# Order of the PSUM banks: the second products of four FFNs and an output projection visit their accumulators bank by bank

## The chip, the cores and the metric

The kernel is one program on one core of a Trainium2 chip. Its engines are TensorE (PE, with its weight load PEld), VectorE (DVE), ScalarE (ACT), GpSimd (POOL) and SyncE (SP), each with a queue of its own that is worked off in order; they wait for each other on semaphores. PE writes its products into PSUM, which has eight banks; a bank holds one tile of 128 x 512 fp32 numbers. The metric is the device time of one execution in microseconds (us), as the median of several runs.

## The reference

A decoder trunk of two layers on one sequence of 256 tokens with 1024 channels, in fp32. Every layer computes

```
h += 1/2 * SwiGLU(RMSNorm(h)); h += Mixer(RMSNorm(h)); h += 1/2 * SwiGLU(RMSNorm(h))
SwiGLU(x) = (silu(x @ w_in[:, :2816]) * (x @ w_in[:, 2816:])) @ w_out
```

The mixer of layer 0 is an S5 state-space mixer. After layer 0 one shared set of keys and values is computed. The mixer of layer 1 is an attention with three branches (16 heads in four groups of four): compressed keys, selected blocks, and a window. The sum of its branches, 256 x 1024, is multiplied by `w_o` (1024 x 1024) and added to h. So the program has four FFNs with inner width 2816, and one output projection of 256 x 1024 by 1024 x 1024.

## The kernel before

**Products.** Tokens are two tiles t of 128 rows. An fp32 product is made of three fp32r matmuls (`mm3`, L112-117): both operands are split into a high part and a low remainder, and hi·hi (L115), hi·lo (L116) and lo·hi (L117) are added in one PSUM bank. The activations stand still in the array (128 x 128), the weights move through (128 x 512).

**Weights.** They arrive by DMA in granules of 1 MB from SP's queue (`load_granule`, two `raw` buffers). `split_half` makes the high part on ACT (`whi`, L86, or L96 with a gain) and the low part on DVE (`wlo`, L92 or L99). The weights `w_o` of the output projection are fetched with `eng='ag'`: there POOL subtracts (`wlo`, L92 on POOL). `whi` and `wlo` have five buffers each that are used in turn, so the cast into a buffer waits until PE has done the last matmul with what the buffer held.

**FFN** (`ffn`, L177-242). The inner width is worked in 11 chunks of 256. For one chunk the first products go to two banks `mm` (one per token tile); ACT and DVE make g = silu · gate of them (L235, L236); PE transposes g (L190), and `split` makes its hi and lo parts `gT` (L140, L141). `second(c, gT)` multiplies by the chunk of `w_out` and adds to `acc2`, four PSUM tiles `o{t}{hf}` (token tile t, half hf of the channels), which stay open over all 11 chunks. It visits them by f (half of the chunk), hf, t; in the last chunk by t, hf, f, since there DVE adds a finished half to h (L214) and `done` starts the next stage. The pool `ps_a` hands out the banks 4, 5, 6, 7 in the order in which the tiles are asked for: o00, o01, o10, o11. In visiting order o00, o10, o01, o11 the banks are 4, 6, 5, 7.

**Attention** (L796-964) is a list of units, `ORD` (L794): queries, `logits` (l), `compressed` (c), `mix` (m) by group and token tile, and `project` (p). `compressed` makes the softmax over the compressed keys: after ACT's exponential (L856) and DVE's normalisation (L862) it splits the weights into `pst` (ACT L140, DVE L141), which PE transposes (`tr<-ident,pst`, L868) and ACT copies into `pcT` (L869). `mix` normalises the weights `Pt` of a token tile by eight DVE operations (L906), transposes them on PE (L913) and multiplies them with the values (L922, L925). The last units are `c3 p0 p2 m30 p4 m31 p6`.

**Projection** (`project`, L933-946). p0, p2, p4, p6 each add two slabs of 128 channels to four accumulators: `acc[0]` is a bank `mm` (0) and a bank `x` (7), `acc[1]` a bank `mm` (1) and a bank `x` (6); the second index is the half n of the channels. A unit visits them by t, n, j (j the slab), that is six matmuls in a row to one bank. After the last unit DVE adds them to h (L945).

**What sets the order.** The code is recorded, and a scheduler orders each engine's queue by modelled times and by `tc.issue_after`; what stands in a row in the program is therefore not what stands in a row in the code, and a small change of one engine's order can change another's. At run time each engine goes through its queue in that fixed order.

Of the kernel before, what the change touches and what calls it, by code (L numbers as in the profile page):

```python
# [9 lines left out]
F32 = mybir.dt.float32  # L10
# [6 lines left out]
P = 128  # L17
D = 1024
KT = D // P
# [13 lines left out]
def kernel(ctx: ExitStack, tc: tile.TileContext, A, out):  # L33
# [16 lines left out]
    def tr_bank():  # L50
        return Banks.tr.tile([P, 512], F32, name=Banks.tag)

    # ---- constants and gains
    h = pers.tile([P, 2, D], F32, name="h")
    ident = pers.tile([P, P], F32, name="ident")
    gains = pers.tile([P, 6, KT], F32, name="gains")
# [4 lines left out]
    nc.sync.dma_start(out=h[:, 0, :], in_=A["x"][0])  # L61
    nc.sync.dma_start(out=gains, in_=A["gains"])

    # ---- weights: each granule is split exactly into hi + lo parts as it arrives, scaled by the gain of its rows
    class Last:
        dma = act = dve = pe = None

# [8 lines left out]
    nc.sync.dma_start(out=raw0[:, 1024:2048], in_=A["w_in1_0"][0, 0][:, 1024:2048])  # L76

    def split_half(raw, j, w, gain, k0, eng="av"):
        """eng: which engines round and subtract"""
        eh, el = ({"a": S, "v": V, "g": G}[x] for x in eng)  # L80
        hi = hip.tile([P, 1024], F32R, name="whi")[:, 0:2 * w]
        lo = lop.tile([P, 1024], F32R, name="wlo")[:, 0:2 * w]
        r = raw[:, j * 2 * w:(j + 1) * 2 * w]
        if gain is None:
            if eh is S:
                Last.act = S.activation(hi, r, AF.Copy)  # L86
            else:
                Last.dve = V.tensor_copy(hi, r)
        for s_ in range(2):
            c = slice(s_ * w, (s_ + 1) * w)  # L90
            if gain is None:
                i = el.tensor_tensor(out=lo[:, c], in0=r[:, c], in1=hi[:, c].bitcast(F32), op=ALU.subtract)  # L92
            else:
                g_ = gains[:, gain, k0 + s_:k0 + s_ + 1]
                if eh is S:
                    Last.act = S.activation(hi[:, c], r[:, c], AF.Identity, scale=g_)  # L96
                else:
                    V.tensor_scalar(out=hi[:, c], in0=r[:, c], scalar1=g_, scalar2=None, op0=ALU.mult)
                i = V.scalar_tensor_tensor(out=lo[:, c], in0=r[:, c], scalar=g_, in1=hi[:, c].bitcast(F32), op0=ALU.mult, op1=ALU.subtract)  # L99
            if el is V:  # L100
                Last.dve = i
        return hi, lo
# [14 lines left out]
        Last.pe = T.matmul(ps, lhsT=xl, rhs=wh, start=False, stop=stop_)  # L117

    def gemm(acc, xT, gen, kts=KT, lead=False):
        """acc[t] = x[t] @ W over kts slabs; lead: token tile 0 goes first in groups of four slabs"""  # L120
        for k0 in range(0, kts, 4):
            ws = [next(gen) for _ in range(4)] if lead else None
            for t_ in range(2) if lead else (None,):
                for k in range(k0, k0 + 4):
                    w = ws[k - k0] if lead else next(gen)
                    for t in ((t_,) if lead else range(2)):
                        mm3(acc[t], xT, k, t, w, k == 0, k == kts - 1)

    # ---- 1/rms of the rows of one token tile of h, from its two halves
    def row_square(hc, t, hf, ss):  # L130
        junk = small.tile([P, 512], mybir.dt.bfloat16, name="junk", bufs=1)
        S.activation(junk, hc[:, t, hf * 512:(hf + 1) * 512], AF.Square, scale=1.0 / 32.0, accum_out=ss[:, 2 * t + hf:2 * t + hf + 1])
# [8 lines left out]
        V.tensor_tensor(out=dst_lo, in0=src, in1=dst_hi.bitcast(F32), op=ALU.subtract)  # L141
        return i

    # ---- h^T as hi and lo parts, channels on partitions, with 1/rms of its rows
    class Acts:
        def __init__(self, hc):
            self.h = hc
# [16 lines left out]
                    row_rstd(u, self.ss, self.rs)  # L164

    def background(bg, n):
        """n steps of other work, queued behind what has been issued so far"""
        if bg is None:
            return
        with ExitStack() as st:  # L170
            for i in (Last.act, Last.dve, Last.dma):
                st.enter_context(tc.issue_after(i.ins))
            for _ in range(n):
                next(bg, None)

    # ---- res += 1/2 SwiGLU(rmsnorm(h)); done(t, half) once a half of token tile t of res is complete
    def ffn(x, gi, w_in, w_out, res, perm=False, bg=None, steps=1, done=None, first=()):  # L177
        with tc.tile_pool(name="ffn", bufs=2) as fp, tc.tile_pool(name="ps_a", bufs=1, space=PSUM) as pa:
            xT, rs = x.xT, x.rs
            acc2 = [[pa.tile([P, 512], F32, name=f"o{t}{hf}") for hf in range(2)] for t in range(2)]  # L180
            g_in = granules([w_in[c, kh] for c in range(NCH) for kh in range(2)], gain=gi, first=first)
            g_out = granules([w_out[j] for j in range(NCH)])

            def transposed(g):
                """g^T of one chunk, hi and lo, tokens in natural order"""
                gT = fp.tile([P, 2, 2, 256], F32R, name="gT")
                ps = tr_bank()
                for f in range(2):
                    for t in range(2):
                        T.transpose(ps[:, (f * 2 + t) * P:(f * 2 + t + 1) * P], g[:, t, f * P:(f + 1) * P], ident)  # L190
                if perm:
                    src = ps.rearrange("p (f t e c) -> p f t e c", f=2, t=2, e=2)
                    hi, lo = (gT[:, i].rearrange("p f (c t e) -> p f t e c", t=2, e=2) for i in range(2))
                    for f in range(2):
                        split(hi[:, f], lo[:, f], src[:, f])
                else:
                    split(gT[:, 0], gT[:, 1], ps.rearrange("p (f c) -> p f c", f=2))
                return gT
# [42 lines left out]
                background(bg, steps)  # L241
            second(NCH - 1, transposed(prev))

    # ---- S5 in chunks of four tokens: discretisation, rotation tables, and stationary operands
    BG1 = 2
    NG = 32
    NC = 64
# [3 lines left out]
    def s5_prepare(kp, sp, W):  # L251
# [34 lines left out]
        yield  # L286

        def exp_parts(x):
            """2^n and exp(r) - 1 with x = n ln2 + r."""
            xc = ts(nt(), x, -87.0, ALU.max, 88.0, ALU.min)  # L290
            t = ts(nt("et"), xc, LOG2E, ALU.mult, MAGIC + 127.0, ALU.add)
            n = ts(nt("en"), t, MAGIC + 127.0, ALU.subtract)
            r = stt(nt(), n, -LN2_HI, xc, ALU.mult, ALU.add)
            r = stt(nt("er"), n, -LN2_LO, r, ALU.mult, ALU.add)
            sc = nt("es")
            V.tensor_scalar(out=sc.bitcast(I32), in0=t.bitcast(I32), scalar1=23, scalar2=None, op0=ALU.logical_shift_left)
            q = ts(nt(), r, 1.0 / math.factorial(8), ALU.mult)
            for k in range(7, 0, -1):
                q = stt(nt(), q, 1.0 / math.factorial(k), r, ALU.add, ALU.mult)
            return sc, q  # L300

        sc, q = exp_parts(ldt)
# [38 lines left out]
            return x.rearrange("p (g c) -> p g c", c=16)  # L341

        def products(x, y, t4_):
            """x_re y_re, x_im y_im, x_re y_im, x_im y_re"""
            for t_, i, j in zip(t4_, (0, 1, 0, 1), (0, 1, 1, 0)):
                tt(t_, x[i], b16(y[j]), ALU.mult, G)

# [114 lines left out]
            ts(W.cosT[:, gs], f, -2.0, ALU.mult, 1.0, ALU.add)  # L462
            yield

    # ---- h += S5(rmsnorm(h)); token 4 c + 2 t + e is in row 64 e + c of token tile t
    class S5In:
        def __init__(self, hc, kp):
            self.h, self.kp, self.hn = hc, kp, None
# [18 lines left out]
    def s5(hc, x, W, kp, done):  # L487
        cosT, sinT, Cw, Wi, WBT, r4 = W.cosT, W.sinT, W.Cw, W.Wi, W.WBT, W.r4
        with tc.tile_pool(name="s5r", bufs=1) as rp, tc.tile_pool(name="s5w", bufs=2) as wp, \
# [14 lines left out]
                return eng.tensor_tensor(out=o, in0=a, in1=b, op=op)  # L504

            def u_transposed(b0, nb):
                """u^T of 2 nb groups of 32 channels"""
                ps = py.tile([P, 512], F32, name="yb")
                for j in range(nb):
                    T.transpose(ps[:, j * P:(j + 1) * P], x.hn[:, b0 + j].rearrange("p a t c -> p (a t c)"), ident)  # L510
# [8 lines left out]
                return last  # L519

            def rotated(cb):
                """the tables of four groups, for the real and the imaginary half"""
                return [x_[:, cb * 4:cb * 4 + 4].unsqueeze(1).to_broadcast([P, 2, 4, NC]) for x_ in (cosT, sinT)]

            def drive(cb):
# [98 lines left out]
                    V.scalar_tensor_tensor(out=hc[:, t, cs], in0=sg, scalar=0.5, in1=hc[:, t, cs], op0=ALU.mult, op1=ALU.add)  # L624
                    done(t, n)

    # ---- shared keys and values
    # columns of kT: selected, compressed, window
    KC, KWN, KW = 256, 272, 528

    class KV:
        pass

    def bias_tables(kp, tp):
        """B[q, h, k] = bias of head h at distance q + 128 - k, -1e30 past the diagonal."""
        rb = tp.tile([32, P], F32, name="rb")
        nc.sync.dma_start(out=rb, in_=A["rel_bias"])
        oh = tp.tile([32, 256], F32, name="oh")
# [16 lines left out]
        yield  # L655

    def head_ss(tp, x, nh):
        """x: [rows, nh * 64] -> sum of squares per head"""
        rows = x.shape[0]
        sq = tp.tile([P, 384], F32, name="sq")[:rows, :nh * 64]  # L660
        G.tensor_tensor(out=sq, in0=x, in1=x, op=ALU.mult)
        ss = tp.tile([P, 8], F32, name="hss")[:rows, :nh]
        V.tensor_reduce(out=ss, in_=sq.rearrange("p (h d) -> p h d", d=64), axis=mybir.AxisListType.X, op=ALU.add)
        return ss
# [22 lines left out]
            G.tensor_copy(KV.kvT[i][:, 4, 0:32:2], pos)  # L687

    def shared_kv(x, kp, tp):
        """the projections; what follows them comes back as a generator"""  # L690
        KV.kT = kp.tile([P, 2, 4, KW], F32R, name="kT")
        KV.V = kp.tile([P, 2, 2, 4, 64], F32, name="Vt")
        KV.Vc = kp.tile([P, 4, 2, 2, 64], F32R, name="Vc")
# [98 lines left out]

        return post()

    # ---- h += NSA(rmsnorm(h))
    ORD = "q0 q1 t0 l00 l01 q2 t1 c0 m00 l10 m01 l11 q3 t2 c1 m10 l20 m11 l21 t3 c2 m20 l30 m21 l31 c3 p0 p2 m30 p4 m31 p6"  # L796

    def attention(x, hc, done):
        with tc.tile_pool(name="at", bufs=1) as ap, tc.tile_pool(name="at2", bufs=2) as tp, \
# [49 lines left out]
                        S.activation(qT[:, h0:h0 + 4, t * P:(t + 1) * P], ps.rearrange("p (h c) -> p h c", c=P), AF.Copy)  # L849

            def compressed(g, lg):
                """softmax over the compressed keys, both token tiles"""
                mx = tp.tile([P, 2, 4], F32, name="cmx")
                V.tensor_reduce(out=mx, in_=lg, axis=mybir.AxisListType.X, op=ALU.max)
                V.tensor_tensor(out=lg, in0=lg, in1=mx.unsqueeze(3).to_broadcast([P, 2, 4, 15]), op=ALU.subtract)
# [77 lines left out]
            def project(k0, k1):  # L933
                if not acc:
                    acc.extend([mm_bank(), x_bank()] for _ in range(2))
                for k in range(k0, k1, 2):
                    ws = [[next(gen) for _ in range(2)] for _ in range(2)]
                    for t in range(2):
                        for n in range(2):
                            for j in range(2):  # L940
                                mm3(acc[t][n], oT, k + j, t, ws[j][n], k + j == 0, k + j == KT - 1)
                        if k + 2 == KT:
                            for n in range(2):
# [173 lines left out]
```

## Time and profile before

| what | value |
|---|---|
| median of 3 runs | 1076.11 us (1074.67 to 1076.71) |
| profiled execution, first to last instruction (span) | 1070.4 us |
| PE busy | 1002.3 us, 94% of the span, 5553 matmuls |
| DVE, ACT, POOL busy | 708.6, 574.7, 180.5 us |
| mean granted TensorE clock | 0.981 |
| attention's end with the projection | about 846 to 878 us of the span |
| last FFN | about 877 us to the end |

The profile gives the profiled execution's span, and no other time for it; the median of the runs is 5.7 us above that span. Rows of groups give an operation as output <- inputs with the number of its instructions and their busy time; matmuls overlap, so the distance of two starts, not the duration in a row, is what one costs. Rows of the timeline have start, duration, engine, line, operation, and in brackets the idle time before it with the instruction that ended it. Rows of windows have a stretch, its length, busy time of each engine (with the number of instructions that started), the granted TensorE clock (1.00 or 0.50 of full speed), the share of DMA time and GB/s.

### The profile page before, as it was taken

Reading aid. Unit: us, or ns where it says so; the run is one execution under the profiler, and the core shown is the slowest. Engines: PE = TensorE matmul, PEld = TensorE weight load, DVE = VectorE, ACT = ScalarE, POOL = GpSimd, SP = SyncE. Lnnn points to the kernel's source line nnn. Section 1 sums busy time; section 2 is a strip of 40 time slices with the busy share of each in tenths; the row PEclk is TensorE's granted clock in tenths of the full one; section 3 lists DMA queues with packets and bytes.
Section 4 is the critical chain, followed back from the end, with each engine's and each line's share of the span. In section 5 each row is a group of like instructions: output and inputs, shape, how many; then the busy total and the mean of one; then the engine's idle time right before and its main releaser. Section 6 shows DMA issues by size and latency. Waiting matters only on the chain.

```text
span 1070.4 us, 14818 instructions
## 1 busy us (share of the span) xinstructions
PE 1002.3 (94%) x5553; PEld 807.9 (75%) x5553; DVE 708.6 (66%) x1403; ACT 574.7 (54%) x1051; POOL 180.5 (17%) x185
## 2 busy tenths in 40 slices
PE   7978999988879899999999999999977899999998
PEld 6766877876657688887887888887866678888886
DVE  5999755949875465656757555655688866656553
ACT  6443566643335464655665555554786656545451
POOL 6375100305732000000005100000203220000000
PEclk9988999999989999999999999999988999999999
DMA  6553544420328865555464455554303146555551
GB/s 237 183 187 118 197 158 140 163 91 24 137 103 205 331 201 193 197 176 181 170 221 158 158 187 173 191 197 145 100 1 118 40 138 214 170 186 197 185 176 72
DMA packets 27912, 171.74 MB, mean 160 GB/s; under 512 B 4544, under 2 KB 4992, under 8 KB 9024
## 3 DMA queue, kind: packets, MB, share of 16 engines
q1 hardware_dynamic: 26192, 164.77, 44.5%
q0 software_dynamic: 1648, 6.03, 2.2%
q8 instruction: 43, 0.70, 0.3%
q14 instruction: 29, 0.24, 0.1%
HBM read 165.54 MB, written 5.24 MB: 160 GB/s over the span
## 4 chain that ended last, share of the span: by engine, by line
PE 73%; DVE 14%; DMA 4%; ACT 4%; POOL 3%; issue 2%; SPq 0%; ACTq 0%; POOLq 0%; DVEq 0%
PE mm L115 14%; PE mm L116 13%; PE mm L117 13%; PE o L117 7%; PE o L115 7%; PE o L116 7%; DMA raw<-in_w_in_dram 4%; DVE wlo L99 4%; DVE wlo L92 2%; PE tr L190 1%; DVE w L544 1%; ACT whi L96 1%; DVE Pt L906 1%; ACT Pt L895 1%; PE tr L913 1%
## 5 line engine op out<-in xcount | busy, mean ns | idle before, releaser
L99 DVE SCALAR_TENSOR_TENSOR wlo<-raw,gains,whi 128x512 fp32r<-128x512 f32 (+2 forms) x408 | 295.7, 759 | 130.6 <-ACT whi L96 126.7
L96 ACT ACTIVATE whi<-raw,gains 128x512 fp32r<-128x512 f32 (+2 forms) x408 | 267.3, 699 | 187.2 <-PE mm L117 60.8
L115 PE MATMUL mm<-whi,xT 128*128 128x512 f32 (+2 forms) x800 | 313.5, 392 | 4.5 <-ACT whi L96 3.5
L117 PE MATMUL mm<-whi,xT 128*128 128x512 f32 (+2 forms) x800 | 307.1, 384 | 0.0
L116 PE MATMUL mm<-wlo,xT 128*128 128x512 f32 (+2 forms) x800 | 306.8, 384 | 0.3 <-DVE wlo L99 0.3
L92 DVE TENSOR_TENSOR wlo<-raw,whi 128x512 fp32r<-128x512 f32 x192 | 135.0, 743 | 95.3 <-ACT whi L86 95.1
L86 ACT ACTIVATE whi<-raw 128x1024 fp32r<-128x1024 f32 x104 | 108.8, 1057 | 133.6 <-PE mm L117 62.1
L115 PEld LDWEIGHTS mm<-whi,xT 128*128 128x128 f32 x800 | 151.1, 189 | 36.0 <-ACT whi L96 4.8
L117 PEld LDWEIGHTS mm<-whi,xT 128*128 128x128 f32 x800 | 150.9, 189 | 29.8
L116 PEld LDWEIGHTS mm<-wlo,xT 128*128 128x128 f32 x800 | 151.2, 189 | 28.4 <-DVE wlo L99 1.1
L115 PE MATMUL o<-whi,gT 128*128 128x512 f32 x352 | 143.0, 406 | 9.5 <-ACT gT L140 9.5
L117 PE MATMUL o<-whi,gT 128*128 128x512 f32 x352 | 141.6, 404 | 8.1 <-DVE gT L141 7.9
L116 PE MATMUL o<-wlo,gT 128*128 128x512 f32 x352 | 141.4, 402 | 0.0
L115 PEld LDWEIGHTS o<-whi,gT 128*128 128x128 f32 x352 | 67.7, 192 | 27.5 <-ACT gT L140 11.9
L117 PEld LDWEIGHTS o<-whi,gT 128*128 128x128 f32 x352 | 67.6, 192 | 26.3 <-DVE gT L141 10.1
L116 PEld LDWEIGHTS o<-wlo,gT 128*128 128x128 f32 x352 | 67.7, 192 | 15.7
L235 ACT ACTIVATE g<-mm,rs 128x256 f32<-128x256 f32 x88 | 40.7, 471 | 27.7 <-PE mm L117 27.6
L236 DVE SCALAR_TENSOR_TENSOR g<-mm,rs,g 128x256 f32<-128x256 f32 x88 | 41.9, 483 | 19.9 <-ACT g L235 19.4
L141 DVE TENSOR_TENSOR gT<-tr,gT 128x512 fp32r<-128x512 f32 (+1 forms) x55 | 36.4, 661 | 25.9 <-ACT gT L140 25.6
L140 ACT ACTIVATE gT<-tr 128x512 fp32r<-128x512 f32 (+1 forms) x55 | 33.3, 605 | 33.4 <-PE tr L190 26.7
L137 POOL TENSOR_TENSOR rs<-ms,nhalf 128x1 f32<-128x1 f32 x12 | 7.2, 600 | 231.7 <-DVE ms L136 231.6
L895 ACT ACTIVATE Pt<-Pt,mx 128x128 f32<-128x128 f32 (+1 forms) x64 | 28.4, 445 | 6.4 <-DVE mx L890 6.3
(311 smaller groups left out, 1009.1 us busy)
## 6 DMA issues: line engine op xcount, KB each, us to landing
raw<-in_w_in_dram SPq DMA_DIRECT2D x87, 1024.0 KB, 4.9
raw<-in_w_out_dram SPq DMA_DIRECT2D x44, 1024.0 KB, 4.9
raw<-in_w_kv_dram SPq DMA_DIRECT2D x6, 1024.0 KB, 4.8
raw<-in_w_glu_dram SPq DMA_DIRECT2D x4, 1024.0 KB, 4.8
raw<-in_w_o_dram SPq DMA_DIRECT2D x4, 1024.0 KB, 4.9
revd<-rev POOLq DMA_DIRECT2D x8, 384.0 KB, 15.0
raw<-in_w_qg_dram SPq DMA_DIRECT2D x6, 512.0 KB, 3.6
B<-revd POOLq DMA_DIRECT2D x1, 2048.0 KB, 13.2
```

Source lines behind the costliest of these rows:

```text
L86: Last.act = S.activation(hi, r, AF.Copy)
L92: i = el.tensor_tensor(out=lo[:, c], in0=r[:, c], in1=hi[:, c].bitcast(F32), op=ALU.subtract)
L96: Last.act = S.activation(hi[:, c], r[:, c], AF.Identity, scale=g_)
L99: i = V.scalar_tensor_tensor(out=lo[:, c], in0=r[:, c], scalar=g_, in1=hi[:, c].bitcast(F32), op0=ALU.mult, op1=ALU.subtract)
L115: T.matmul(ps, lhsT=xh, rhs=wh, start=start, stop=False)
L116: T.matmul(ps, lhsT=xh, rhs=wl, start=False, stop=False)
L117: Last.pe = T.matmul(ps, lhsT=xl, rhs=wh, start=False, stop=stop_)
L140: i = S.activation(dst_hi, src, AF.Copy)
L141: V.tensor_tensor(out=dst_lo, in0=src, in1=dst_hi.bitcast(F32), op=ALU.subtract)
L235: Last.act = S.activation(sl, acc[t][:, 0:256], AF.Silu, scale=rs[:, t:t + 1])
L236: Last.dve = V.scalar_tensor_tensor(out=g[:, t, :], in0=acc[t][:, 256:512], scalar=rs[:, t:t + 1], in1=sl, op0=ALU.mult, op1=ALU.mult)
L895: S.activation(Pt[:, r, br], Pt[:, r, br], AF.Exp, scale=-1.0, bias=mx[:, c:c + 1], accum_out=sm[:, c:c + 1])
```

## The change

In `ffn` the four accumulators are asked for in the order o00, o10, o01, o11, so that the banks of the usual visiting order are 4, 5, 6, 7; in the last chunk, whose order in the code is unchanged, they are then 4, 6, 5, 7. In `project` all units but the last visit by j, n, t, so that three matmuls in a row go to one bank and the banks follow as 0, 1, 7, 6; the last visits by t, j, n.

```
-            acc2 = [[pa.tile([P, 512], F32, name=f"o{t}{hf}") for hf in range(2)] for t in range(2)]
+            acc2 = list(zip(*[[pa.tile([P, 512], F32, name=f"o{t}{hf}") for t in range(2)] for hf in range(2)]))
...
                     ws = [[next(gen) for _ in range(2)] for _ in range(2)]
+                    if k + 2 < KT:
+                        for j in range(2):
+                            for n in range(2):
+                                for t in range(2):
+                                    mm3(acc[t][n], oT, k + j, t, ws[j][n], k + j == 0, False)
+                        continue
                     for t in range(2):
-                        for n in range(2):
-                            for j in range(2):
+                        for j in range(2):
+                            for n in range(2):
                                 mm3(acc[t][n], oT, k + j, t, ws[j][n], k + j == 0, k + j == KT - 1)
```

The rest of the diff drops comments and docstrings, by which line numbers behind them move by one in the attention. The number of instructions of every kind is unchanged. What follows are places where the instructions of an engine stand in another order; names are output <- inputs, and the number behind a name counts the uses of tiles over the program.

PE, in an ordinary chunk of an FFN. The number of an `o` is the order in which it was asked for, so 3101 to 3104 are the banks 4 to 7. Before:

```order
L115 MATMUL o00_3101<-whi_3690,gT_3649 128x512
L116 MATMUL o00_3101<-wlo_3691,gT_3649 128x512
L117 MATMUL o00_3101<-whi_3690,gT_3649 128x512
L115 MATMUL o10_3103<-whi_3690,gT_3649 128x512
L116 MATMUL o10_3103<-wlo_3691,gT_3649 128x512
L117 MATMUL o10_3103<-whi_3690,gT_3649 128x512
L115 MATMUL o01_3102<-whi_3690,gT_3649 128x512
```

After:

```order
L115 MATMUL o00_3101<-whi_3690,gT_3649 128x512
L116 MATMUL o00_3101<-wlo_3691,gT_3649 128x512
L117 MATMUL o00_3101<-whi_3690,gT_3649 128x512
L115 MATMUL o10_3102<-whi_3690,gT_3649 128x512
L116 MATMUL o10_3102<-wlo_3691,gT_3649 128x512
L117 MATMUL o10_3102<-whi_3690,gT_3649 128x512
L115 MATMUL o01_3103<-whi_3690,gT_3649 128x512
```

The products, their operands and their order are the same; the second group goes to bank 5 where it went to bank 6, and the third the other way.

PE, at the first matmuls of p0 and p2 into the banks `x`: x_7613 is bank 7 (token tile 0), x_7615 bank 6 (token tile 1); whi_7618 and whi_7623 are the slabs of p0, whi_7654 and whi_7659 those of p2. Before:

```order
L115 MATMUL x_7613<-whi_7618,oT_6522 128x512
L116 MATMUL x_7613<-wlo_7619,oT_6522 128x512
L117 MATMUL x_7613<-whi_7618,oT_6522 128x512
L115 MATMUL x_7613<-whi_7623,oT_6522 128x512
L116 MATMUL x_7613<-wlo_7624,oT_6522 128x512
L117 MATMUL x_7613<-whi_7623,oT_6522 128x512
L115 MATMUL x_7615<-whi_7618,oT_6522 128x512
L116 MATMUL x_7615<-wlo_7619,oT_6522 128x512
L117 MATMUL x_7615<-whi_7618,oT_6522 128x512
```

After:

```order
L115 MATMUL x_7613<-whi_7618,oT_6522 128x512
L116 MATMUL x_7613<-wlo_7619,oT_6522 128x512
L117 MATMUL x_7613<-whi_7618,oT_6522 128x512
L115 MATMUL x_7615<-whi_7618,oT_6522 128x512
L116 MATMUL x_7615<-wlo_7619,oT_6522 128x512
L117 MATMUL x_7615<-whi_7618,oT_6522 128x512
L115 MATMUL x_7613<-whi_7623,oT_6522 128x512
L116 MATMUL x_7613<-wlo_7624,oT_6522 128x512
L117 MATMUL x_7613<-whi_7623,oT_6522 128x512
```

The last use of whi_7618 is the ninth of these matmuls before and the sixth now. Likewise the last use of whi_7654 was behind the transposes of `pst1` and is now ahead of them; those transposes stand behind 17 of the matmuls of p0 and p2 before and behind 20 now.

ACT, at the same place. whi_7728 takes the buffer of whi_7618, whi_7810 that of whi_7623, whi_7815 that of whi_7654. Before:

```order
L856 ACTIVATE clg_7459<-clg_7459 128x120
L86 ACTIVATE whi_7728<-raw_7721 128x1024
L140 ACTIVATE pst1_6526<-clg_7459 128x8x15
L86 ACTIVATE whi_7810<-raw_7808 128x1024
L869 ACTIVATE pcT_6523<-tr_7606 128x2x256
L86 ACTIVATE whi_7815<-raw_7808 128x1024
```

After:

```order
L857 ACTIVATE clg_7459<-clg_7459 128x120
L86 ACTIVATE whi_7728<-raw_7721 128x1024
L86 ACTIVATE whi_7810<-raw_7808 128x1024
L140 ACTIVATE pst1_6526<-clg_7459 128x8x15
L86 ACTIVATE whi_7815<-raw_7808 128x1024
L870 ACTIVATE pcT_6523<-tr_7606 128x2x256
```

Two casts moved forward by one place, past the high part of `pst1` and past the copy into `pcT`.

DVE, at the same place. Before:

```order
L906 TENSOR_SCALAR Pt1_7547<-Pt1_7547,sm_7549 128x256
L862 TENSOR_TENSOR clg_7459<-clg_7459,csm_7598 128x120
L906 TENSOR_SCALAR Pt1_7547<-Pt1_7547,sm_7549 128x256 x3
L141 TENSOR_TENSOR pst1_6526<-clg_7459,pst1_6526 128x8x15
L906 TENSOR_SCALAR Pt1_7547<-Pt1_7547,sm_7549 128x256 x2
L916 COPY pt1_7711<-tr_7706 128x512
```

After:

```order
L907 TENSOR_SCALAR Pt1_7547<-Pt1_7547,sm_7549 128x256
L863 TENSOR_TENSOR clg_7459<-clg_7459,csm_7598 128x120
L907 TENSOR_SCALAR Pt1_7547<-Pt1_7547,sm_7549 128x256 x5
L141 TENSOR_TENSOR pst1_6526<-clg_7459,pst1_6526 128x8x15
L917 COPY pt1_7711<-tr_7706 128x512
```

The low part of `pst1` now stands behind all five remaining normalisations of `Pt1`, two places later. POOL's order is the same: six subtractions for whi_7728, whi_7810 and whi_7815 in a row.

## The prediction

> **What bounds the kernel now.** I read the page first, then the windows of the last FFN and of the whole middle, then the starts of single matmuls, and last the timeline of PE, ACT, DVE and POOL around the projection. From the page:
>
> ```profile
> PE 1002.3 (94%) x5553; PEld 807.9 (75%) x5553; DVE 708.6 (66%) x1403; ACT 574.7 (54%) x1051; POOL 180.5 (17%) x185
> L115 PE MATMUL o<-whi,gT 128*128 128x512 f32 x352 | 143.0, 406 | 9.5 <-ACT gT L140 9.5
> ```
>
> From the windows of the last FFN:
>
> ```profile
> 877.65:1059.00 181.35, 181.35 (x815) 148.32 (x814) 105.66 (x163) 97.14 (x146) 1.12 (x2) 1.00 0.51 174
> ```
>
> PE is busy 94% of the span, and for 181.35 of 181.35 us in the last FFN, at full clock. So two things can move the time: what one matmul costs, and a wait of PE. A delay ahead of the last FFN is not made good in it, since PE has no idle time there to give back.
>
> What one matmul costs is read from starts, twelve matmuls apart: first products; an ordinary block of second products (banks 4, 6, 5, 7, three matmuls each); the closing block (the start of its last matmul on bank 5, then six on bank 6 and five on 7). The last pair is the product `ga` of the S5 mixer, six apart, which also goes through the banks 4, 5, 6, 7, but with `xT` as the stationary operand.
>
> ```profile
> 1042.84 0.39 PE L115 MATMUL mm<-whi,xT 128*128 128x512 f32 x1
> ...
> 1045.57 0.39 PE L115 MATMUL mm<-whi,xT 128*128 128x512 f32 x1
> ...
> 1056.11 0.39 PE L117 MATMUL o<-whi,gT 128*128 128x512 f32 x1
> ...
> 1058.91 0.40 PE L117 MATMUL o<-whi,gT 128*128 128x512 f32 x1
> ...
> 1063.10 0.40 PE L117 MATMUL o<-whi,gT 128*128 128x512 f32 x1
> ...
> 1065.90 0.40 PE L117 MATMUL o<-whi,gT 128*128 128x512 f32 x1
> ```
>
> ```profile
> 271.96 0.39 PE L117 MATMUL ga<-whi,xT 128*128 128x512 f32 x1
> ...
> 273.32 0.39 PE L117 MATMUL ga<-whi,xT 128*128 128x512 f32 x1
> ```
>
> The pitches are 2.73/12 = 227.5 ns for `mm`, 2.80/12 = 233.3 ns for `o` with banks that lie two apart, 2.80/12 = 233.3 ns for `o` six in a row and then a neighbouring bank, and 1.36/6 = 226.7 ns for `ga`. The pitch of `o` is the same in both orders of banks, and `ga` has the low pitch on the same four banks. What differs is the stationary operand, `gT` against `xT`, and the change leaves that.
>
> **Part 1: the banks of the second products.** The four FFNs have 4 x 11 x 24 = 1056 matmuls into `o` (352 for each of three lines, by the page); the order stays, half of them change their bank. The bounds: if neighbouring banks gave all that the first products have, 1056 x (233.3 − 226.7) ns = −7.0 us. On the side of a loss, the closing blocks, in which the banks go two apart now, have 4 x 24 = 96 matmuls, and the whole of the same difference on them would be +0.6 us. I take 0, because the closing block before is already the case with neighbours alone, and it has the pitch of the ordinary one. The additions to h after it (L214) go to the same tiles in the same order.
>
> **Part 2: the projection.** Three matmuls in a row to a bank instead of six: by the same rows 0. What counts is when buffers come free. The rows of PE, ACT, DVE and POOL around p0 and p2:
>
> ```profile
> 852.67 0.40 PE L117 MATMUL x<-whi,oT 128*128 128x512 f32 x1
> ...
> 853.38 0.39 PE L117 MATMUL x<-whi,oT 128*128 128x512 f32 x1
> ...
> 855.25 0.40 PE L116 MATMUL x<-wlo,oT 128*128 128x512 f32 x1
> 856.48 0.66 PE L868 MATMUL tr<-ident,pst 128*128 128x128 f32 x4 [0.84 <-DVE pst L141]
> 856.89 0.47 PE L117 MATMUL x<-whi,oT 128*128 128x512 f32 x1
> ...
> 859.38 0.48 PE L115 MATMUL mm<-whi,oT 128*128 128x512 f32 x1
> 859.93 0.65 PE L922 MATMUL s<-pt,Vt 128*64 128x256 f32 x4
> ```
>
> ```profile
> 853.81 1.06 ACT L86 ACTIVATE whi<-raw 128x1024 fp32r<-128x1024 f32 x1 [1.18 <-PE x L117]
> 854.77 0.29 ACT L140 ACTIVATE pst<-clg 128x120 fp32r<-128x120 f32 x1
> 854.97 1.04 ACT L86 ACTIVATE whi<-raw 128x1024 fp32r<-128x1024 f32 x1
> ```
>
> ```profile
> 854.24 0.88 DVE L906 TENSOR_SCALAR Pt<-Pt,sm 128x256 f32<-128x256 f32 x3
> 855.09 1.33 DVE L141 TENSOR_TENSOR pst<-clg,pst 128x120 fp32r<-128x120 f32 x1
> 856.35 2.67 DVE L906 TENSOR_SCALAR Pt<-Pt,sm 128x256 f32<-128x256 f32 x2
> ```
>
> ```profile
> 855.01 7.63 POOL L92 TENSOR_TENSOR wlo<-raw,whi 128x512 fp32r<-128x512 f32 x6 [21.11 <-ACT whi L86]
> ```
>
> The cast of whi_7728 at 853.81 waited for the last matmul with whi_7618, the one at 853.38. In the new order that is the sixth of them, the one that started at 852.67 (0.71 us sooner): the cast starts at 853.10. POOL's six subtractions began 0.14 us after that cast's end (853.81 + 1.06 = 854.87) and would begin at 854.30. One of them takes 7.63/6 = 1.27 us, so they end at 855.57, 856.84, 858.11, 859.38, 860.66 and 861.93. The casts of whi_7810 and whi_7815 come early enough for no gap: their buffers are free after the twelfth and the eighteenth of these matmuls, about 854.5 and 855.9.
>
> Now DVE. Alone, a normalisation takes 0.88/3 = 0.29 us. While POOL subtracts, DVE gets one operation done for each of POOL's: `pst` took 1.33 us and ended 0.14 us after POOL's first operation (856.28), and the next two normalisations took 2.67 us. Another place shows the same, with seven normalisations against two subtractions, and that POOL gets in while DVE has a row of them before it:
>
> ```profile
> 808.87 4.06 DVE L906 TENSOR_SCALAR Pt<-Pt,sm 128x256 f32<-128x256 f32 x7
> ```
>
> ```profile
> 808.89 2.56 POOL L92 TENSOR_TENSOR wlo<-raw,whi 128x512 fp32r<-128x512 f32 x2 [17.51 <-PE mm L117]
> ```
>
> [...]
>
> In the new order five normalisations, from 854.24 on, stand ahead of the low part of `pst`. One is under way when POOL starts at 854.30; the second to the fifth each wait for the end of one subtraction (855.57, 856.84, 858.11, 859.38), and `pst` for the fifth (860.66) and 0.14 us more: 860.80, where it ended at 856.42. PE's four transposes of `pst`, 0.06 us behind, move from 856.48 to 860.86, by +4.38 us. PE works in order, so all behind them waits; ahead of them now stand three more matmuls, −0.70 us (3 x 234 ns), which otherwise come behind. PE would be idle from about 856.3 to 860.86.
>
> **What such a wait does to the clock.** A wait of that length stands in the same stage before, for the `pst` of another group:
>
> ```profile
> 812.73 0.50 PE L115 MATMUL mm<-whi,oT 128*128 128x512 f32 x1
> 817.75 0.66 PE L868 MATMUL tr<-ident,pst 128*128 128x128 f32 x2 [4.52 <-DVE pst L141]
> ```
>
> ```profile
> 101.53:104.94 3.41, 2.74 (x7) 2.16 (x8) 3.41 (x6) 0.00 (x0) 2.12 (x2) 0.50 0.72 279
> 104.94:108.36 3.42, 3.42 (x10) 2.65 (x9) 2.81 (x4) 1.93 (x5) 3.42 (x3) 0.50 0.32 60
> 811.50:814.92 3.42, 1.64 (x7) 0.89 (x5) 2.56 (x11) 1.18 (x3) 0.91 (x1) 1.00 0.00 0
> 814.92:818.33 3.41, 0.58 (x3) 0.61 (x4) 2.58 (x8) 0.82 (x2) 2.61 (x4) 0.50 0.00 0
> 818.33:821.74 3.41, 3.41 (x17) 2.66 (x15) 2.53 (x9) 2.80 (x12) 0.69 (x1) 0.50 0.46 135
> 855.88:859.29 3.41, 2.81 (x18) 2.46 (x19) 3.14 (x3) 1.79 (x4) 3.41 (x4) 1.00 0.31 46
> ```
>
> ```profile
> 58.23 0.63 PE L115 MATMUL o<-whi,gT 128*128 128x512 f32 x1
> ...
> 59.51 0.63 PE L115 MATMUL o<-whi,gT 128*128 128x512 f32 x1
> ```
>
> The granted clock changes in steps of 3.41 us, the stretches of these windows: after one with PE busy 1.64 of 3.42 us the next runs at 0.50, after one with 2.74 at half clock it stays at 0.50. At half clock a matmul costs 1.28/3 = 427 ns. If the steps lie as they do in this run, 855.88 to 859.29 would have PE busy for 0.4 us only; 859.29 to 862.70 then runs at half clock, is busy for 1.8 us of it, and so 862.70 to 866.11 runs at half clock too. From 860.86 to 866.11 that is 5.25 us at 234/427 of the speed: +2.4 us. Against that, some small waits of before vanish, such as the 0.55 us between the starts of 859.38 and 859.93 where a matmul otherwise costs 0.23: −0.3 us, and as much again (an estimate from this one) in the second mix, whose order is alike.
>
> **The sum:** 4.4 − 0.7 + 2.4 − 0.6 = +5.5 us. The profiled span of 1070.4 us becomes 1075.9; the median of the runs shown lies 5.7 us above the span, and the same shift on 1076.11 gives 1081.6 us. What a measurement can tell from no change is about 0.2%, 2.15 us.
>
> Bounds of the shift: if the normalisation at 854.24 is caught as well, `pst` waits for all six subtractions, +1.3 us of wait that falls where the clock is low, about +6.6 in all (1082.7), and with a step of the clock in an unlucky place 1 us more. If the steps lie so that half clock costs one window instead of one and a half, 0.8 us less; if the clock stays at full, 5.5 − 2.4 = +3.1 (1079.2).
>
> **Rivals.**
> - *The banks do set the pitch.* Then the second products gain up to 7.0 us, and with the new wait in the projection the time is 1076.1 − 7.0 + 5.5 = 1074.6; it ends faster by over 0.2% only where the gain is above 2.2 us and the wait is absent (1069.1), or above 7.6 us with it. Against it stand the two `o` blocks of 2.80 us above. Nor does PE's clock suffer from a change of banks from group to group: in the long middle, which is full of both kinds of products, it is granted in full.
>
> ```profile
> 360.90:784.00 423.10, 414.41 (x1977) 341.87 (x1975) 261.03 (x470) 241.47 (x411) 24.23 (x32) 1.00 0.52 179
> ```
>
> - *POOL doesn't get in between.* DVE runs its five normalisations at 0.29 us each from 854.24 to 855.7, and `pst` waits for one subtraction at most: it ends at 856.98 instead of 856.42, with three matmuls of 0.70 us moved ahead of it. The shift is 0.56 − 0.70 = −0.1 us, 1076.0: no change. For it speaks that the order of starts within a tenth of a microsecond decides; against it 808.87 and 808.89, where POOL got in 0.02 us after a row of seven had begun.
> - *The wait is there, the clock stays.* 1079.2, as above. Against it the rows at 811.50 and 814.92, where a like wait was followed by half clock although PE was busy for 1.64 us of the first of the two stretches. [...]
>
> **Chances.** The wait with half clock, at 1080.2 to 1083.7: 0.65. The wait without it, or shorter by one or two subtractions: 0.14, of which 0.02 stay within 0.2%. No wait: 0.13, no change. Banks set the pitch: 0.08, of which 0.06 are faster by over 0.2%. Faster by over 0.2%: 0.06; within: 0.02 + 0.13 + 0.02 = 0.17, the last 0.02 being small gains of the banks; slower: the rest, 0.77. The range from 1077.6 to 1083.7 leaves out the cases with no wait or with a gain, and holds those with a wait.
>
> **What would show it.** In the profile of the changed kernel: an idle time of 4 to 5 us ahead of `tr<-ident,pst` in the projection, ended by DVE's `pst`, where 0.84 us stood; five normalisations in a row that take 5 to 6 us beside POOL's subtractions; a window or two at 0.50 right behind; the pitch of `o` at 233.3 ns in ordinary and closing blocks alike; the last FFN as long as before. Wrong would make it: a pitch of `o` that differs from before, a wait ahead of `pst` below 2 us, or waits in other stages, where no instruction has moved.

## The result, and the profile after

| | before | changed |
|---|---|---|
| median of 22 runs each | 1075.82 us (1072.27 to 1079.43) | 1082.89 us (1077.44 to 1088.18) |
| ratio, 95% interval | | 1.0062 (1.005 to 1.0075) |
| profiled execution, span | 1070.4 us | 1082.8 us |
| PE busy | 1002.3 us | 1010.9 us |
| mean granted TensorE clock | 0.981 | 0.969 |

The change makes the kernel 7.1 us slower by the medians (5.4 to 8.1 by the interval). For the changed kernel a time is known beside the profile's span: the profiled execution took 1084.54 us, 1.74 us more than its span. With the same 1.74 us the profiled execution of before took about 1072.1 us (an estimate), a little below the fastest of its 22 runs. The two profiled spans therefore differ by 12.4 us, more than the medians. The timelines say where: p0's first `x` matmul starts at 851.51 before and at 857.66 now, so 6.15 us arose ahead of the projection. In that part no instruction has moved, only banks have other numbers (what they cost is experiment e5), while the stretches at half clock fall otherwise in the two executions: ahead of that matmul there are 12 windows of 3.41 us at half clock in the profile of before and 17 in that of the changed kernel. The mean clocks in the table are those of these two executions. The median over executions is 0.975 for before (57 of them, run beside the experiments, 0.966 to 0.982) and 0.971 for the changed kernel (22); a difference of 0.004 is about two and a half windows at half clock (0.004 x 1080 / 0.5 / 3.41, an estimate), not seven. What follows is read inside the projection.

The start of p0's `x` matmuls in the timeline of before:

```profile
851.51 0.39 PE L115 MATMUL x<-whi,oT 128*128 128x512 f32 x1
```

The timeline of PE in the changed kernel, from that matmul on:

```profile
857.66 0.39 PE L115 MATMUL x<-whi,oT 128*128 128x512 f32 x1
...
862.09 0.40 PE L116 MATMUL x<-wlo,oT 128*128 128x512 f32 x1
867.18 1.11 PE L869 MATMUL tr<-ident,pst 128*128 128x128 f32 x4 [4.69 <-DVE pst L141]
867.94 0.78 PE L117 MATMUL x<-whi,oT 128*128 128x512 f32 x1
```

ACT, DVE and POOL there, up to 866 us:

```profile
859.25 1.06 ACT L86 ACTIVATE whi<-raw 128x1024 fp32r<-128x1024 f32 x1 [0.49 <-PE x L117]
860.70 1.06 ACT L86 ACTIVATE whi<-raw 128x1024 fp32r<-128x1024 f32 x1 [0.39 <-PE x L117]
861.67 0.29 ACT L140 ACTIVATE pst<-clg 128x120 fp32r<-128x120 f32 x1
```

```profile
860.38 5.48 DVE L907 TENSOR_SCALAR Pt<-Pt,sm 128x256 f32<-128x256 f32 x5
865.78 1.34 DVE L141 TENSOR_TENSOR pst<-clg,pst 128x120 fp32r<-128x120 f32 x1
```

```profile
860.46 6.52 POOL L92 TENSOR_TENSOR wlo<-raw,whi 128x512 fp32r<-128x512 f32 x5 [20.40 <-ACT whi L86]
```

POOL's row goes on behind the edge of this view: all six subtractions take 7.79 us, 1.30 us each. POOL starts 0.08 us after DVE's row of five, which then takes 5.48 us where five at 0.29 us would take 1.5; `pst` comes out at 867.12 and PE has waited 4.69 us instead of 0.84. The windows of the same stretch, and the last FFN (columns as before: busy time of PE, PEld, DVE, ACT, POOL, clock, DMA):

```profile
862.30:865.71 3.41, 0.18 (x1) 0.00 (x0) 3.41 (x3) 0.87 (x1) 3.41 (x4) 1.00 0.41 101
865.71:869.13 3.42, 1.95 (x7) 1.76 (x8) 1.41 (x2) 0.60 (x1) 2.54 (x3) 0.50 0.49 206
869.13:872.54 3.41, 3.41 (x14) 2.49 (x14) 0.80 (x2) 1.21 (x2) 0.00 (x0) 0.50 0.83 308
872.54:875.95 3.41, 3.41 (x19) 2.17 (x16) 1.49 (x3) 1.54 (x3) 0.00 (x0) 1.00 0.00 0
889.65:1071.00 181.35, 181.35 (x815) 148.34 (x814) 105.92 (x164) 97.17 (x146) 1.12 (x2) 1.00 0.51 174
```

Two windows at half clock follow the wait, of which PE uses 867.18 to 872.54, 5.36 us. The last row stands beside 877.65:1059.00 of before: the same 815 matmuls in the same 181.35 us, PE busy throughout. Nothing is lost or won there. And the pitch of `o`, in an ordinary chunk (22 apart) and in the closing block (13 apart):

```profile
1065.91 0.40 PE L115 MATMUL o<-whi,gT 128*128 128x512 f32 x1
...
1071.04 0.40 PE L116 MATMUL o<-wlo,gT 128*128 128x512 f32 x1
...
1075.00 0.40 PE L115 MATMUL o<-whi,gT 128*128 128x512 f32 x1
...
1078.03 0.39 PE L116 MATMUL o<-wlo,gT 128*128 128x512 f32 x1
```

5.13/22 = 233.2 ns and 3.03/13 = 233.1 ns, against 233.3 before.

### The profile page after: what moved, and what is told of

It is laid out like the page before. It is cut to its first block, busy times and chain, and to the rows that moved or that the text cites. A ratio compares the mean times of both kernels' runs of the same rounds, so it can differ in the third digit from the quotient of the medians.

```text
span 1082.8 us, 14818 instructions
## 1 busy us (share of the span) xinstructions
PE 1010.9 (93%) x5553; PEld 815.0 (75%) x5553; DVE 711.1 (66%) x1403; ACT 575.6 (53%) x1051; POOL 179.9 (17%) x185
## 4 chain that ended last, share of the span: by engine, by line
PE 73%; DVE 14%; ACT 4%; DMA 3%; POOL 3%; issue 2%; SPq 0%; ACTq 0%; POOLq 0%; DVEq 0%
PE mm L115 13%; PE mm L116 13%; PE mm L117 13%; PE o L115 7%; PE o L117 7%; PE o L116 7%; DVE wlo L99 3%; DMA raw<-in_w_in_dram 3%; DVE wlo L92 2%; DVE Pt L907 1%; PE tr L191 1%; ACT whi L96 1%; PE tr L914 1%; ACT Pt L896 1%; PE dr L530 1%
## 5 line engine op out<-in xcount | busy, mean ns | idle before, releaser
L117 PEld LDWEIGHTS o<-whi,gT 128*128 128x128 f32 x352 | 68.0, 193 | 28.7 <-DVE gT L141 12.4
## 6 DMA issues: line engine op xcount, KB each, us to landing
revd<-rev POOLq DMA_DIRECT2D x8, 384.0 KB, 14.8
```

## The experiments

Theory A is that of the prediction: p0's order frees a buffer sooner, POOL's subtractions begin ahead of DVE's normalisations and hold DVE up, PE waits for `pst`, and the clock drops. Rival B is that the order of banks costs by itself. Rival C is that `pst` is late by its place in the queues, whatever POOL does. A last group of runs asks what the difference of 7 us between the two kinds of products is, which had been the bound of a gain.

**e1, the new order for p0 alone.**

```
                     ws = [[next(gen) for _ in range(2)] for _ in range(2)]
+                    if k == 0:
+                        for j in range(2):
+                            for n in range(2):
+                                for t in range(2):
+                                    mm3(acc[t][n], oT, k + j, t, ws[j][n], k + j == 0, False)
+                        continue
```

> Of the change only the new visiting order of p0 is kept; the FFNs' banks and p2, p4, p6 are as before. ACT's and DVE's order around pst becomes that of the changed kernel. Theory A (buffer of p0's first slab comes free sooner, POOL's subtractions start ahead of the normalisations and hold up DVE): idle time of 4 to 5 us ahead of the transposes of pst, half clock right behind, time 5.5 to 7.1 us above before (ratio 1.005 to 1.0066). Rival B (the banks' order, spread over 1056 second products and 96 of the projection, makes the loss): p0 is 24 of 1152 matmuls, so under 0.2 us and no wait.

Measured: 1.0034 (1.0016 to 1.0051), 1079.89 against 1076.75 us. DVE's row, PE's transposes and the windows there:

```profile
858.68 5.47 DVE L906 TENSOR_SCALAR Pt<-Pt,sm 128x256 f32<-128x256 f32 x5
864.07 0.27 DVE L141 TENSOR_TENSOR pst<-clg,pst 128x120 fp32r<-128x120 f32 x1
```

```profile
864.40 1.11 PE L868 MATMUL tr<-ident,pst 128*128 128x128 f32 x4 [3.62 <-DVE pst L141]
```

```profile
860.42:863.84 3.42, 0.36 (x2) 0.00 (x0) 3.42 (x3) 0.00 (x0) 3.42 (x3) 1.00 0.37 98
863.84:867.25 3.41, 2.85 (x10) 2.36 (x11) 0.50 (x2) 1.55 (x2) 0.24 (x2) 0.50 0.50 209
867.25:870.67 3.42, 3.42 (x24) 2.35 (x23) 1.97 (x3) 1.75 (x4) 2.43 (x2) 1.00 0.00 0
```

24 matmuls in another order bring the wait back, so B is out as the main cause. The size is below what was expected, 3.1 us instead of 5.5 to 7.1. Here whi_7815's cast stays behind the copy into `pcT` in ACT's order, so POOL has four subtractions in a row instead of six. The five normalisations take as long as in the whole change, but no fifth subtraction stands beside `pst`, which takes 0.27 us instead of 1.34: the wait is 3.62 us instead of 4.69. And in this execution half clock lasts for one window, in which PE was busy for 2.85 of 3.41 us, and not for two.

**e2, the whole change except p0.** As the changed kernel, with p0 in the old loops t, n, j.

```
+                    if k == 0:
+                        for t in range(2):
+                            for n in range(2):
+                                for j in range(2):
+                                    mm3(acc[t][n], oT, k + j, t, ws[j][n], k + j == 0, False)
+                        continue
                     if k + 2 < KT:
```

> The whole change except p0, which is visited as before. Theory A: ACT's and DVE's order around pst is that of before, the wait there is 0.8 us or less, and the time is that of before within 0.15% (1.5 us). Rival B: nearly the whole loss stays, 6 to 7 us (ratio 1.0055 to 1.0065).

Measured: 1.0022 (1.0006 to 1.0038). The wait ahead of `pst` is 0.85 us, about as A says, but by the medians 2.2 us remain where A expected no more than 1.5; A missed there. The trace has a new wait 12 us later, in the mix m31, and half clock behind it (PE, ACT, windows):

```profile
868.42 0.40 PE L116 MATMUL mm<-wlo,oT 128*128 128x512 f32 x1
870.65 0.65 PE L923 MATMUL s<-pt,Vt 128*64 128x256 f32 x4 [1.84 <-ACT pt L919]
```

```profile
869.39 0.72 ACT L96 ACTIVATE whi<-raw,gains 128x512 fp32r<-128x512 f32 x1 [2.60 <-DMA raw<-in_w_in_dram]
870.02 0.58 ACT L919 ACTIVATE pt<-tr 128x512 f32<-128x512 f32 x1
```

```profile
867.95:871.36 3.41, 1.57 (x11) 0.75 (x10) 1.21 (x2) 1.82 (x3) 0.00 (x0) 1.00 0.88 300
871.36:874.77 3.41, 3.41 (x14) 1.82 (x16) 1.16 (x3) 0.60 (x1) 0.00 (x0) 0.50 0.14 58
```

In before the copy `pt` stands ahead of the cast that waits for this DMA:

```profile
866.39 0.58 ACT L918 ACTIVATE pt<-tr 128x512 f32<-128x512 f32 x1
867.66 1.33 ACT L96 ACTIVATE whi<-raw,gains 128x512 fp32r<-128x512 f32 x2 [0.70 <-DMA raw<-in_w_in_dram]
```

The new order of p2, p4 and p6 puts a cast of the last FFN's weights ahead of the copy `pt` on ACT, and the cast waits for its DMA. In the whole change the same place comes later by the wait at `pst`: there the same cast waits for PE only and PE's wait is gone. So the two halves of the projection's change don't add up as waits; one covers the other. One trace shows this second wait; whether it stands in every execution of e2 is open.

**e3, the changed kernel without POOL's reads.** The low parts of w_o's last four slabs are zeros (this part of the computation is left out).

```
-                i = el.tensor_tensor(out=lo[:, c], in0=r[:, c], in1=hi[:, c].bitcast(F32), op=ALU.subtract)
+                if el is G and Last.cut:
+                    i = G.memset(lo[:, c].bitcast(F32), 0.0)
+                else:
+                    i = el.tensor_tensor(out=lo[:, c], in0=r[:, c], in1=hi[:, c].bitcast(F32), op=ALU.subtract)
...
```

`Last.cut` is set for the last two of the four granules of w_o.

> The changed kernel, but the low parts of the last four slabs of w_o (of p4 and p6) are left out: POOL writes zeros there instead of subtracting, so it reads nothing from SBUF. PE's order is the same, and ACT's and DVE's around pst are too. Theory A: the five normalisations take 1.5 to 2 us instead of 5.5, the wait ahead of the transposes of pst is under 1 us, no half clock behind it, time within 0.2% of before. Rival C (pst is late because its place in DVE's queue is behind five normalisations, or because ACT's cast goes first, whatever POOL does): the wait stays above 3 us and the time 5 us above before.

Measured: 0.9999 (0.9981 to 1.0018). With the order of the changed kernel around `pst`, DVE, POOL and PE there:

```profile
857.05 2.23 DVE L911 TENSOR_SCALAR Pt<-Pt,sm 128x256 f32<-128x256 f32 x5
859.21 0.27 DVE L145 TENSOR_TENSOR pst<-clg,pst 128x120 fp32r<-128x120 f32 x1
```

```profile
856.27 1.14 POOL L94 MEMSET wlo<- 128x512 f32 x2 [0.26 <-PE x L120]
857.67 1.22 POOL L94 MEMSET wlo<- 128x512 f32 x2 [0.26 <-PE x L120]
```

```profile
859.53 0.66 PE L873 MATMUL tr<-ident,pst 128*128 128x128 f32 x4 [1.29 <-DVE pst L145]
```

```profile
855.36:858.77 3.41, 2.89 (x13) 2.00 (x11) 3.41 (x10) 2.87 (x4) 2.89 (x6) 1.00 0.47 135
858.77:862.18 3.41, 2.65 (x17) 2.16 (x17) 0.86 (x4) 1.29 (x4) 0.11 (x1) 1.00 0.99 372
```

Five normalisations take 2.23 us instead of 5.48, the wait is 1.29 us (a little over the 1 us expected), the clock stays, and the loss is gone. C is out: the places in the queues are the same. POOL's zeros still slow DVE somewhat: five at 0.29 us would take 1.5. A zero write takes about 0.6 us and a subtraction 1.30, so e3 changes the length of POOL's operations together with their reads and doesn't tell the two apart. The second wait, in m31, is absent here: the same cast starts at 868.21, 14.8 us after p0's first `x` matmul against 16.2 in e2, and PE doesn't wait. POOL's zeros don't read `raw`, so the trace can't say whether subtractions without the first wait would leave it absent too.

**e5, the banks of the FFNs alone.** The first two lines of the diff, the projection as before.

> The FFNs' half of the change alone: the four accumulators on banks 4, 5, 6, 7 in visiting order, the projection as before. Theory A: pitch of o 233.3 ns as before, no new wait, time that of before within 0.15%. Rival B (the banks make part of the loss, by the 0.2% that was left without p0): ratio 1.002 or above, and a pitch of o above 234 ns or new idle time ahead of an o.

Measured: 1.0003 (0.9988 to 1.0019), 1075.38 against 1075.48 us. The pitch of `o` in its trace is 5.36/23 = 233.0 ns (1039.78 to 1045.14), and PE's waits in the attention are those of before within 0.1 us. The FFNs' half of the change does nothing that can be measured, and the loss is the projection's.

**e10 and e11, the whole change where no POOL subtraction is.** Both have gT next to xT (e4 below) and `eng='av'` for w_o, so that DVE subtracts; e10 has the change on top.

```
-            gen = granules([A["w_o"][j] for j in range(KT // 2)], eng='ag')
+            gen = granules([A["w_o"][j] for j in range(KT // 2)], eng='av')
```

> The whole change on the base with gT next to xT and w_o's low parts on DVE, where no POOL subtraction stands beside the normalisations. Theory A: the change costs nothing there: the difference to that base is within 0.2% (2 us), and no wait of over 1.5 us ahead of pst in the projection. If the order in the projection costs by itself, it is 4 us or more above that base.

> That base once more, on the same chip as the run before it: ratio to before 0.985 to 0.9885, as its first measurement (0.9868).

Measured: e10 0.9857 (0.9834 to 0.988), 1059.96 us; e11 0.9863 (0.9843 to 0.9883), 1061.45 us. The difference is within the intervals, so the change costs nothing that can be measured on this base, and e10's transposes of `pst` in the projection start with no idle time ahead of them. All arithmetic is kept here, but the queues around `pst` are others: three short normalisations of 128x128 stand directly ahead of its low part in e10 and six in e11, not five of 128x256. So these runs show that the visiting order costs nothing measurable by itself; that the places in the queues aren't the cause rests on e3.

**e4 and e6, gT next to xT.**

```
     pers = ctx.enter_context(tc.tile_pool(name="pers", bufs=1))
+    gtp = ctx.enter_context(tc.tile_pool(name="gtp", bufs=2))
     rawp = ctx.enter_context(tc.tile_pool(name="rawp", bufs=2))
-    hip = ctx.enter_context(tc.tile_pool(name="hip", bufs=5))
-    lop = ctx.enter_context(tc.tile_pool(name="lop", bufs=5))
+    hip = ctx.enter_context(tc.tile_pool(name="hip", bufs=4))
+    lop = ctx.enter_context(tc.tile_pool(name="lop", bufs=4))
...
-                gT = fp.tile([P, 2, 2, 256], F32R, name="gT")
+                gT = gtp.tile([P, 2, 2, 256], F32R, name="gT")
```

> Not of the change: the bound of 7.0 us came from the pitch of the second products (233.3 ns) against that of the first (226.7 ns). Before's kernel with gT placed next to xT in SBUF (41.8 to 50 KB of the partition instead of above 146 KB); to make room whi and wlo have four buffers each instead of five, so the whole time isn't compared. If the place of the stationary operand makes the difference, the pitch of o goes to about 227 ns; if it is the kind of product or the bank, it stays at 233 ns.

> The kernel with gT next to xT, timed. The pitch of its second products was 226.8 ns; 1056 matmuls by 6.6 ns less are 7.0 us: time 1069 to 1070 us (ratio 0.993 to 0.994) if four buffers instead of five for whi and wlo cost nothing, above 1072 if they do.

The timeline of e4 in the last FFN, 22 matmuls apart on the banks 4, 6, 5, 7 of before:

```profile
1032.50 0.39 PE L116 MATMUL o<-whi,gT 128*128 128x512 f32 x1
...
1037.49 0.39 PE L117 MATMUL o<-wlo,gT 128*128 128x512 f32 x1
```

4.99/22 = 226.8 ns: the place of the operands makes the difference, not the bank or the kind of product. (`whi` and `wlo` move too, by 8 and 4 KB.) Timed, it is 0.9912 (0.9899 to 0.9924), 1065.74 against 1075.48 us, which is below the 1069 to 1070 us expected; 1056 x 6.5 ns = 6.9 us of these 9.7 are the pitch of `o`. The other 2.8 are not accounted for (the buffers' number changes orders in the attention too).

**e7 and e9, where the place matters.** e7 moves xT from 25 to 84 KB, e9 puts whi below xT.

```
+    xtp = ctx.enter_context(tc.tile_pool(name="xtp", bufs=1))
...
-            self.xT = pers.tile([P, 2, KT, 256], F32R, name="xT")
+            self.xT = xtp.tile([P, 2, KT, 256], F32R, name="xT")
...
```

```
+    hip = ctx.enter_context(tc.tile_pool(name="hip", bufs=5))
     pers = ctx.enter_context(tc.tile_pool(name="pers", bufs=1))
     rawp = ctx.enter_context(tc.tile_pool(name="rawp", bufs=2))
-    hip = ctx.enter_context(tc.tile_pool(name="hip", bufs=5))
```

> The reverse: before's kernel with xT moved up from 25 KB to 84 KB of the partition (raw, whi and wlo move down by 16 KB). If the pitch grows with the stationary operand's distance from the start of SBUF, or from the moving operand, the first products rise above 227 ns, at 233 ns at most; if only places above 100 KB are dear, they stay at 226.7 ns.

> Of the pitch again: whi lies below xT now (16.5 to 37 KB against 45.9 to 62.3 KB), wlo above it (78.7 KB on); gT stays above all. If the pitch goes by whether the stationary operand lies below the moving one, the first products with whi (two of three) go to about 233 ns and those with wlo stay at 227; if it goes by the stationary operand's place alone (near the start of SBUF), all stay at 226.7 ns.

The timelines of the first products, 24 apart in e7 and 27 apart in e9:

```profile
1034.47 0.39 PE L116 MATMUL mm<-whi,xT 128*128 128x512 f32 x1
...
1040.07 0.39 PE L116 MATMUL mm<-whi,xT 128*128 128x512 f32 x1
```

```profile
1017.22 0.39 PE L117 MATMUL mm<-whi,xT 128*128 128x512 f32 x1
...
1023.47 0.39 PE L117 MATMUL mm<-whi,xT 128*128 128x512 f32 x1
```

e7: 5.60/24 = 233.3 ns, so the first products take on the dear pitch at 84 KB already. e9: 6.25/27 = 231.5 ns. That is near the mean of the first reading, (2 x 233 + 227)/3 = 231.0, but not its parts: in this view the distance behind `wlo`'s matmuls is 230.0 ns on average, and 233.3 and 231.1 behind the two with `whi`. The second products of e9 have 5.32/23 = 231.3 ns (1028.33 to 1033.65) although `gT` stayed, so the moving operand's place counts as well as the stationary one's; by what rule is open. (`xT` moves in e9 too, from 25 to 46 KB.) Each of the two ran once, at 1081.98 and 1081.13 us.

**e8, on e6, w_o's low parts on DVE.** The same edit as in e11, timed for the first time.

> As the kernel with gT next to xT, with the low parts of w_o made on DVE instead of POOL. If POOL's subtractions hold DVE up throughout the attention, the waits of PE ahead of pst there (4.5 us and 0.8 us in before) fall below 1 us in all and the time falls 3 to 7 us below the kernel with gT next to xT; if DVE is too full for the 16 subtractions of 0.74 us, the attention gets longer by up to 12 us.

Measured: 0.9868 (0.9852 to 0.9884), 1060.79 us, 5.0 us below e6 on the same chip. The largest sums of PE's waits in the attention, first of e6, then of e8 (us in total, times, longest):

```profile
PE tr L869 <- DVE hms L670: 3.7, 1, 3.7
PE s L885 <- DVE clg L893: 3.4, 2, 1.8
PE tr L869 <- DVE pst L142: 2.8, 2, 2.6
PE s L923 <- DVE pt L917: 1.8, 1, 1.8
```

```profile
PE tr L869 <- DVE clg L893: 3.0, 1, 3.0
PE s L885 <- DVE clg L893: 2.8, 2, 1.6
PE x L923 <- ACT pt L919: 0.5, 1, 0.5
```

No wait for `pst` is left, and DVE has room for the subtractions. e8 (and e10, which is the same within what can be told) is faster than both kernels, 1.3% below before.

## Why the prediction was right

The forecast was 1081.6 us, a shift of +5.5, between 1077.6 and 1083.7; measured are 1082.89 us and +7.1 (5.4 to 8.1). Step by step:

- **The pitch, taken at 0.** Right: 233.2 and 233.1 ns, and e5 gives 1.0003. The bound of −7.0 us was a real difference, but of the operands' places (e4, e9), where the prediction had put it down to the stationary operand as such.
- **The cast starts 0.71 us sooner, POOL 0.14 us behind it.** Right: the rows of after have the cast at 859.25, 1.59 us after p0's first `x` matmul, where before it came 2.30 us after it. The next cast waited, too, for PE's twelfth matmul, as forecast, and POOL's row of six came without a gap: 7.79 us against 7.63.
- **`pst` waits for five subtractions, +4.38 us.** From p0's first `x` matmul to the transposes it was 856.48 − 851.51 = 4.97 us before and 867.18 − 857.66 = 9.52 now: +4.55. e3 shows that it is POOL's subtractions that hold DVE up, and e10 that without them the order costs nothing measurable on its base. Five normalisations took 5.48 us beside subtractions of 1.30 us and 2.23 us beside zeros of about 0.6. That each operation of the row but the first waits for one subtraction was the author's estimate from two places of before; 0.29 + 4 x 1.30 = 5.49 us agrees with the 5.48, and by what means POOL's operations hold DVE's up no run shows. Two things came together here, POOL's earlier start and the two normalisations that the scheduler put ahead of `pst`. By the prediction's list of ends, three normalisations instead of five would let `pst` end at 858.11 + 0.14 = 858.25 instead of 860.80, so 2.55 of the 4.38 us would hang on those two (an estimate; no run has the one without the other).
- **Half clock, +2.4 us; three matmuls, −0.7; small waits, −0.6.** Half clock lasted 5.36 us of PE's work, forecast 5.25, after a window busy for 0.18 us and through one busy for 1.95. That the windows lay so was a supposition that came true: a step comes 862.30 − 857.66 = 4.64 us after p0's first `x` matmul, 855.88 − 851.51 = 4.37 in before, but 855.36 − 853.42 = 1.94 in e3. From the transposes to the first matmul of the last FFN it was 877.65 − 856.48 = 21.17 us before and 889.65 − 867.18 = 22.47 now: +1.30, against the +1.1 of these three terms together; the runs don't separate them.
- **The sum.** Inside the projection the two traces give 4.55 + 1.30 = +5.85 us, forecast +5.5. The medians differ by 1.2 us more, within the interval. The median clocks of 0.975 and 0.971 fit two windows of half clock in the projection and perhaps part of a third elsewhere; the runs don't settle whether the 1.2 us are that or scatter.
- **What lies around the span.** The prediction put 5.7 us between the span and the median of the runs. By the changed kernel's result 1.7 us lie around the span; the other 4 were a profiled execution that was faster than the median. The shift was added to the median, so the forecast did not suffer.
- **Rivals.** That POOL doesn't get in between fell at 860.46: POOL started 0.08 us after DVE's row, which took 5.48 us all the same. That the order of starts within a tenth of a microsecond decides, as that rival had it, no run shows. That the clock stays fell with the windows: 0.18 us of work in the first window did not keep the clock up, and 1.95 us in the second did not bring it back.

What the prediction missed is the second wait in m31 that e2 shows. It named small waits of the second mix as vanishing, and did not see that the new order of p2, p4 and p6 sets a cast that depends on a DMA ahead of `pt`. In the whole change the first wait covers it; it shows in e2, where the first wait is avoided, and not in e3, where POOL leaves `raw` unread.

## What to carry to other kernels

A new order of products that leaves every operation in place can still change when buffers come free, and by that the queues of engines that it never mentions; compare the queues of all engines around each buffer that is handed on, and look what starts earlier, not only what gets later. Before a pass over bank orders, take the pitch of two groups that differ in the bank alone: here six in a row and banks in turn both had 233.3 ns, which settled 1056 matmuls without a run. Where POOL's subtractions of 1.30 us ran beside a row of five short DVE operations, the row took 5.48 us instead of 1.5 (five at 0.29); such a row on a critical path is worth looking for.

## What was not expected

- The pitch of a 128x512 matmul at full clock was 226.8 or 233.3 ns by the place of its operands in SBUF: `gT` above 146 KB gave 233.3, at 42 to 50 KB 226.8; `xT` at 25 KB 227.5, at 84 KB 233.3; with `whi` moved below `xT` 231.5. The rule behind it is open.
- POOL writing zeros, which reads nothing, still slowed DVE: five normalisations took 2.23 us where five at 0.29 us would take 1.5.
- Half clock was not released by a window in which PE was busy for 1.95 of 3.42 us, and was by one busy for 2.85 of 3.41 us (e1). No threshold of busy time follows from this: in the changed kernel two windows at half clock (244.47 to 251.30) with PE busy throughout (19 and 45 matmuls) were followed by half clock again, and at full clock a window of before busy for 1.72 of 3.41 us (268.78 to 272.19) was followed by full clock, where one busy for 1.79 (275.61 to 279.02) was not.
